# Half of the prompt rows' output projection moves into the attention of the sample rows, half between attention and merge

## The chip, the core and the metric

The kernel runs on one core of a Trainium2 chip. The metric is the device time of one execution in microseconds (us); before the change its median over three runs is 3195.66 us (3191.10 to 3197.16). The engines are called by their short names: PE multiplies matrices (PEld loads its stationary operand), DVE is the vector engine, ACT the scalar engine, POOL the general one, and SP issues all DMA transfers of this kernel, in the order in which they stand in its queue.

## The reference, cut to what matters

One layer of an encoder runs over two requests with the same weights, a prompt of 512 rows and a sample of 1024 rows. Each row goes through a mixer with two branches, and then through a feed-forward network:

```python
att = diff_attention(q, k, v, lam, rel_bias)          # softmax over all rows of the same request
att = rmsnorm(att, subln_w) * (1.0 - lam_init)         # per head
y_ssm = rmsnorm(y, ssm_norm_w)                         # the other branch
g = jax.nn.sigmoid(gates.reshape(b, S, 2, D_MODEL))
merged = g[:, :, 0] * (att @ w_proj_attn) + g[:, :, 1] * (y_ssm @ w_proj_ssm)
m = merged @ w_out                                     # the output projection
x = x + rmsnorm(m, norm_post_mix)
h = rmsnorm(x, norm_pre_ffn)                           # goes into the feed-forward network
```

All of it is in float32. D_MODEL is 1024; there are 8 heads of 2 x 64 columns. `x`, `w_out` and the other weights come from memory and the two outputs go back there.

## The kernel before, in words

The 1536 rows are three chunks of 512: chunk 0 is the prompt, chunks 1 and 2 the sample. Each float32 operand of a large product is split into a rounded part and the rest (`split`, line 133: ACT writes the first, DVE or POOL subtracts for the second), and `gemm` (line 164) issues three matmuls for each 128 rows of the contracted dimension, at lines 167, 168 and 169. A product of 1024 x 1024 weights comes in panels of 256 columns (`split_panel`, line 147), of which two fit (tags `whi`, `wlo`, two buffers each); their raw halves go through two buffers of tag `wraw`.

Engines take their instructions in order. That order is not the order of the text alone: the framework places the instructions by dependences, program order and its own estimate of times, and what it decided is seen in the built program.

Around the change there are these stages, by the code of the kernel before:

- **Attention of the sample** (lines 800 to 869). `heads` runs 8 heads; each has 8 blocks of 128 query rows. For a block PE makes the scores (tile `s`, lines 293 and 294), DVE adds the bias and finds the minimum (296), ACT takes the exponential (299), DVE combines the two maps (302 to 304), PE transposes (308, tile `t`), ACT and DVE split the transposed map (311, 312), and PE multiplies it with the values (tile `o`, 256 columns wide). After 4 blocks ACT copies `o` to `av` (319), SP stores it to `att_d` (320), and a mean square follows later (`mean_square`, tile `ms`, lines 323 to 327).
- **Side work** (`side_work`, line 837) is a generator, and `run` (line 210) takes one step of it for each two steps of the attention (`RATIO` 0.5). It has 32 steps: 8 for the gated projection of the prompt's attention and 24 for the gated projection of the other branch. They write `part_d`; their matmuls go to the tile `f`, one PSUM buffer.
- **Scaling** (`att_scale`, line 330). From the mean squares of all heads DVE works out one factor for each row and head, PE transposes them (tile `rt`, 341), DVE copies (343), SP stores them to `r_d` (344).
- **Output projection of the prompt** (`out_proj`, line 1040, for `m0`): 4 panels of `w_out` times 4 blocks of rows, each 24 matmuls of 256 columns. Its operand is `part_d` of chunk 0, loaded and split by `load_merged` (line 886). ACT copies each result and takes its square sum (1048, 1050).
- **Merge of chunk 1** (`merge`, line 895). `load_att` (346) loads for each of 8 heads the attention result and its factors from `r_d` (351, 349; three buffers `araw`), multiplies (352) and splits. Then 8 blocks of 24 matmuls of 512 columns, each gated and added to `part_d` (905 to 913).
- **Norms of chunk 0** (`norms`, line 1053): two normalizations of the projected prompt rows (1066, 1067, 1068, 1074), 32 transposes (1078), ACT evictions (1080) and stores to `h2_d`, beside the next output projection (`m1`). Merge and projection of chunk 2 and the feed-forward network follow.

Of the kernel before, what the change touches and what calls it, by code (L numbers as in the profile page):

```python
# [10 lines left out]
F32 = mybir.dt.float32  # L11
I32 = mybir.dt.int32
F32R = mybir.dt.float32r
AF = mybir.ActivationFunctionType
ALU = mybir.AluOpType
# [3 lines left out]
P = 128  # L19
D = 1024  # L20
KB = D // P
# [12 lines left out]
OT = ("gt", 2)  # L34
NG = 2
YE = ("act_pool",) * 4
RATIO = 0.5
QS = 0
IA = 1
AHEAD = (0,)  # L40
# [37 lines left out]
def hybrid_trunk_kernel(ctx: ExitStack, tc: tile.TileContext, a: dict, y_prompt, y_sample):  # L78
# [5 lines left out]
    def f(ap):  # L84
        return ap.bitcast(F32)
# [26 lines left out]
    r_d = [dram.tile([32 * n, P], F32, name=f"r_d{n}") for n in (1, 2)]  # L112
    m_d = dram.tile([D, 512], F32, name="m_d")
    part_d = dram.tile([D, T], F32, name="part_d")
    x2_d = dram.tile([T, D], F32, name="x2_d")
    h2_d = dram.tile([D, T], F32, name="h2_d")
    ff_d = [dram.tile([DFF, 768], F32, name=f"ff_d{g}") for g in range(2)]
# [29 lines left out]
    def split_panel(*srcs, eng="act_dve"):  # L147
        hi = wp.tile([P, KB, 256], F32R, tag="whi", name="whi")
        lo = wp.tile([P, KB, 256], F32R, tag="wlo", name="wlo")
        n = 256 // len(srcs)  # L150
        for s in (slice(0, 4), slice(4, 8)):
            raw = rp.tile([P, 4, 256], F32, tag="wraw", name="wraw")
            for i, src in enumerate(srcs):
                load(out=raw[:, :, i * n:(i + 1) * n], in_=src.rearrange("(a p) c -> p a c", p=P)[:, s])
            split(hi[:, s], lo[:, s], raw[:], eng)
        return hi, lo
# [173 lines left out]
    def att_scale(g, zq, msq, pool, psp, ptag):  # L330

        n = zq.shape[-1]
        r, t = [pool.tile([P, 8, n], F32, tag=t_, name=t_, bufs=1) for t_ in ("att_r", "att_t")]
        V.reciprocal(t, zq)
        V.tensor_mul(zq, msq, t)
        V.tensor_mul(zq, zq, t)
        V.tensor_scalar(zq, zq, 1.0, EPS, op0=ALU.mult, op1=ALU.add)
        rsqrt(r[:], zq[:], msq[:])
        V.tensor_mul(r, r, t)
        ps = psp.tile([P, 512], F32, tag=ptag, name="rt")  # L340
        TE.transpose(ps[0:8 * n, 0:P], r[:].rearrange("p h j -> p (h j)"), ident)
        rt = pool.tile([P, P], F32, tag="att_rt", name="rt", bufs=1)
        V.tensor_copy(rt[0:8 * n], ps[0:8 * n, 0:P])
        store(out=r_d[g][:], in_=rt[0:8 * n])
# [452 lines left out]

    ap = ctx.enter_context(tc.tile_pool(name="ap", bufs=1, reuse_waits="tile"))
    zq, msq = [ap.tile([P, 8, 8], F32, name=n) for n in ("zq", "msq")]
    with ExitStack() as ph2:  # L800
        qr = ph2.enter_context(tc.tile_pool(name="qr", bufs=2, reuse_waits="tile"))
        qk = ph2.enter_context(tc.tile_pool(name="qk", bufs=2, reuse_waits="tile"))
        pp = ph2.enter_context(tc.tile_pool(name="pp", bufs=2, reuse_waits="tile"))
        at = ph2.enter_context(tc.tile_pool(name="at", bufs=2, reuse_waits="tile"))
        yt = ph2.enter_context(tc.tile_pool(name="yt", bufs=2, reuse_waits="tile"))
        s_ps = ph2.enter_context(tc.tile_pool(name="s_ps", bufs=2, space=PSUM, reuse_waits="tile"))
        t_ps = ph2.enter_context(tc.tile_pool(name="t_ps", bufs=2, space=PSUM, reuse_waits="tile"))
        o_ps = ph2.enter_context(tc.tile_pool(name="o_ps", bufs=1, space=PSUM, reuse_waits="tile"))
        f_ps = ph2.enter_context(tc.tile_pool(name="f_ps", bufs=1, space=PSUM, reuse_waits="tile"))

        pend = []
        def panel(w_):
            w = wp.tile([P, 2, KB, P], F32R, tag="whi", name="whi")
            raw = rp.tile([P, KB, P], F32, tag="wraw", name="wraw")
            load(out=raw, in_=w_.rearrange("(a p) c -> p a c", p=P))
            split(w[:, 0], w[:, 1], raw[:], "act_dve")
            return w[:, 0], w[:, 1]

        def gated(r0, g0, cs, w, act):
            gt = yt.tile([P, 512], F32, tag="gt", name="gt")  # L820
            load(out=gt, in_=g_d[g0 + r0:g0 + r0 + P, cs])
            S.activation(out=gt, in_=gt, func=AF.Tanh, scale=0.5)
            ps = f_ps.tile([P, 512], F32, tag="f", name="f")
            gemm_fm(ps, w, slice(0, P), act)
            V.scalar_tensor_tensor(gt, gt, 1.0, ps, op0=ALU.add, op1=ALU.mult)
            return gt

        def y_rows(c):
            if c == NCH:
                return []  # L830
            v = yT_d[:, c * 512:(c + 1) * 512].rearrange("(a p) t -> p a t", p=P)
            raws = [wp.tile([P, 4, 512], F32, tag="wlo", name="yraw") for _ in range(2)]
            for raw, k in zip(raws, (0, 4)):
                load(out=raw, in_=v[:, k:k + 4])
            return raws

        def side_work():
            ahead = y_rows(0)
            aTt = yt.tile([P, 2, KB, 512], F32R, tag="yT", name="aTt", bufs=1)
            load_att(0, (aTt[:, 0], aTt[:, 1]), lambda: [t_[:, i] for t_ in [rp.tile([P, 2, 512], F32, tag="wraw", name="wraw")]  # L840
                                                 for i in range(2)])
            for r0 in range(0, D, P):
                gt = gated(r0, 0, slice(0, 512), panel(a["w_proj_attn"][0][:, r0:r0 + P]), (aTt[:, 0], aTt[:, 1]))
                store(out=m_d[r0:r0 + P, :], in_=gt)
                yield

            for c in range(NCH):
                cs = slice(c * 512, (c + 1) * 512)
                yTt = yt.tile([P, 2, KB, 512], F32R, tag="yT", name="yTt", bufs=1)
                for i_, raw in enumerate(ahead):  # L850
                    for j in (0, 2):
                        k = i_ * 4 + j
                        split(yTt[:, 0, k:k + 2], yTt[:, 1, k:k + 2], raw[:, j:j + 2], YE[k // 2])
                ahead = y_rows(c + 1)
                for r0 in range(0, D, P):
                    gt = gated(r0, D, cs, panel(a["w_proj_ssm"][0][:, r0:r0 + P]), (yTt[:, 0], yTt[:, 1]))
                    if c == 0:
                        mt = rp.tile([P, 512], F32, tag="wraw", name="mt")
                        load(out=mt, in_=m_d[r0:r0 + P, :])
                        G.tensor_add(gt, gt, mt)  # L860
                    store(out=part_d[r0:r0 + P, cs], in_=gt)
                    yield

        side = side_work()
        run(heads(512, 1024, range(8), pend, zq, msq, qk, pp, at, qr, s_ps, t_ps, o_ps),
            side, RATIO)
        for _ in side:
            pass
        pend.pop()()


    with ExitStack() as ph3:
# [9 lines left out]

        def big_pair():
            return [big.tile([P, KB, 512], F32R, tag="big", name="big") for _ in range(2)]

        def load_merged(c):
            hi, lo = big_pair()
            for k in range(0, KB, 2):
                both = mp.tile([P, 2, 512], F32, tag="mt", name="both", bufs=4)
                load(out=both, in_=part_d[k * P:(k + 2) * P, c * 512:(c + 1) * 512].rearrange("(a p) t -> p a t", p=P))  # L890
                S.activation(out=hi[:, k:k + 2], in_=both, func=AF.Copy, scale=0.5)
                V.scalar_tensor_tensor(lo[:, k:k + 2], both, 0.5, f(hi[:, k:k + 2]), op0=ALU.mult, op1=ALU.subtract)
            return hi, lo

        def merge(c, aTt):
            cs = slice(c * 512, (c + 1) * 512)
# [138 lines left out]
        with ExitStack() as ph3a:  # L1035
# [4 lines left out]
            def out_proj(mT):  # L1040
                tiles = [mp.tile([P, D], F32, tag="mt", name="mt", bufs=4) for _ in range(4)]
                sums = wk.tile([P, 4, 4], F32, tag="ms4", name="ms4")
                for p0 in range(0, D, 256):
                    w = split_panel(a["w_out"][0][:, p0:p0 + 256])
                    for j in range(4):
                        ps = mm_tile(256)
                        gemm_tm(ps, w, mT, slice(j * P, (j + 1) * P))
                        S.copy(tiles[j][:, p0:p0 + 256], ps)
                        sq = wk.tile([P, 256], F32, tag="gt", name="msq")
                        S.activation(out=sq, in_=ps, func=AF.Square, accum_out=sums[:, j, p0 // 256:p0 // 256 + 1])  # L1050
                return tiles, sums
# [32 lines left out]
                return load_att(c, big_pair(), lambda: [  # L1084
                    wk.tile([P, 512], F32, tag="araw", name="araw", bufs=3) for _ in range(2)])

            m0 = load_merged(0)
            att_scale(1, zq, msq, ap, tr_ps, "tr")
            aT1 = att(1)
            t0 = out_proj(m0)  # L1090
            m1 = merge(1, aT1)
            norms(0, t0)
            aT2 = att(2)
# [118 lines left out]
```

## Time and profile before

| | us |
|---|---|
| median of 3 runs | 3195.66 |
| profiled execution | 3197.76 |
| its span, first to last instruction | 3196.0 |
| PE busy in the span | 3044.8 (95%) |
| DVE busy | 1837.5 (57%) |
| ACT busy | 1256.7 (39%) |

The share of PE is that of the whole program; the stages around the change differ from it, and so the rows below take them one by one. A PE row's duration holds the pipeline's depth, so matmuls overlap: what a matmul costs in a stream is the distance from one start to the next. The granted clock of PE is given as a share of 2.4 GHz.

### The profile page before, as it was taken

How to read it: one execution, taken by the hardware profiler on the slowest of the kernel's cores; microseconds unless marked ns; L12 is line 12 of the kernel's file. 1: busy time of each engine (PE TensorE's matmuls, PEld its weight loads, DVE VectorE, ACT ScalarE, POOL GpSimd, SP SyncE). 2: the span in 40 equal slices, each digit the busy share in tenths (PEclk: the TensorE clock that was granted, in tenths of full speed). 3: DMA queues.
4: the chain of work that ended last, by engine and by line, in shares of the span. 5: the costliest groups of instructions: out<-in, count | busy, mean ns of one | idle time of the engine just before them, and what ended most of it. 6: DMA issues, size and time to landing. Idle time of an engine off the chain costs nothing. (4 is left out here: it accounts for less than half of the span.)

```text
span 3196.0 us, 44151 instructions
## 1 busy us (share of the span) xinstructions
PE 3044.8 (95%) x16667; PEld 2677.0 (84%) x16667; DVE 1837.5 (57%) x2953; ACT 1256.7 (39%) x2301; POOL 681.7 (21%) x520
## 2 busy tenths in 40 slices
PE   8999999999999999899999898978999899989998
PEld 7988887888887777788888787878999899978787
DVE  5214444455327996387878955686667765632444
ACT  4103333333303333366666645543333333332343
POOL 0001111000133442243332100023333433210100
PEclk9999999999999999999999999989999999999999
DMA  4633333123554444755546047644333333363454
GB/s 149 195 99 113 112 104 106 57 79 106 152 170 136 147 143 149 212 173 167 165 137 186 27 139 239 218 141 136 103 98 105 97 103 91 114 203 97 124 163 132
DMA packets 443165, 430.35 MB, mean 135 GB/s; under 512 B 25232, under 2 KB 360305, under 8 KB 441841
## 3 DMA queue, kind: packets, MB, share of 16 engines
q1 hardware_dynamic: 442953, 427.55, 43.3%
q8 instruction: 131, 2.15, 0.3%
q14 instruction: 81, 0.66, 0.1%
HBM read 315.40 MB, written 120.44 MB: 136 GB/s over the span
## 5 line engine op out<-in xcount | busy, mean ns | idle before, releaser
L167 PE MATMUL acc<-hT,whi 128*128 128x512 f32 x1056 | 421.4, 399 | 4.0 <-ACT st L453 4.0
L168 PE MATMUL acc<-hT,whi 128*128 128x512 f32 x1056 | 416.7, 395 | 0.0
L169 PE MATMUL acc<-hT,wlo 128*128 128x512 f32 x672 | 262.2, 390 | 0.0
L167 PEld LDWEIGHTS acc<-hT,whi 128*128 128x128 f32 x1056 | 199.0, 188 | 50.2 <-issue 5.8
L299 ACT ACTIVATE pt<-pt,nm 128x1024 f32<-128x1024 f32 (+1 forms) x192 | 193.1, 1006 | 109.9 <-DVE nm L296 106.6
L168 PEld LDWEIGHTS acc<-hT,whi 128*128 128x128 f32 x1056 | 199.1, 189 | 42.7 <-issue 3.6
L296 DVE CUSTOM_DVE_ANT_0 pt<-s,tb 128x1024 f32<-128x1024 f32 (+1 forms) x192 | 197.5, 1041 | 52.4 <-PE s L294 40.4
L167 PE MATMUL acc<-whi,hT 128*128 128x256 f32 x768 | 225.2, 293 | 1.2 <-DVE st L374 0.6
L169 PE MATMUL acc<-whi,hT 128*128 128x256 f32 x768 | 225.6, 294 | 0.5 <-DVE hT L207 0.3
L168 PE MATMUL acc<-wlo,hT 128*128 128x256 f32 x768 | 224.2, 292 | 0.0
L169 PE MATMUL d<-dhi,fl 128*128 128x512 f32 x528 | 207.8, 393 | 8.9 <-DVE fl L136 8.9
L167 PE MATMUL d<-dhi,fh 128*128 128x512 f32 x528 | 207.7, 393 | 6.8 <-ACT fh L135 6.8
L168 PE MATMUL d<-dlo,fh 128*128 128x512 f32 x528 | 207.1, 392 | 0.0
L135 ACT CAST whi<-wraw 128x1024 fp32r<-128x1024 f32 (+1 forms) x115 | 115.9, 1036 | 213.8 <-PE acc L169 83.1
L136 DVE TENSOR_TENSOR fl<-raw,fh 128x896 fp32r<-128x896 f32 (+1 forms) x72 | 86.0, 1195 | 198.1 <-ACT fh L135 190.2
L234 POOL TENSOR_TENSOR ql<-raw,qh 128x512 fp32r<-128x512 f32 x48 | 65.3, 1373 | 577.3 <-ACT qh L231 567.9
L167 PE MATMUL mm<-op,wy 128*128 128x384 f32 x528 | 178.8, 339 | 9.5 <-ACT op L135 7.3
L169 PE MATMUL mm<-op,wy 128*128 128x384 f32 x528 | 178.6, 338 | 0.0
L168 PE MATMUL mm<-op,wy 128*128 128x384 f32 x528 | 178.3, 338 | 0.0
L136 DVE TENSOR_TENSOR wlo<-wraw,whi 128x1024 fp32r<-128x1024 f32 x80 | 97.1, 1243 | 114.9 <-ACT whi L135 105.6
L135 ACT CAST fh<-raw 128x896 fp32r<-128x896 f32 (+1 forms) x72 | 70.8, 983 | 225.8 <-PE d L168 189.9
L167 PEld LDWEIGHTS acc<-whi,hT 128*128 128x128 f32 x768 | 148.3, 193 | 12.1 <-issue 10.0
(358 smaller groups left out, 8325.0 us busy)
## 6 DMA issues: line engine op xcount, KB each, us to landing
wraw<-in_w_in_dram SPq DMA_DIRECT2D x60, 512.0 KB
wraw<-in_w_gate_up_dram SPq DMA_DIRECT2D x92, 256.0 KB
raw<-ff_d SPq DMA_DIRECT2D x48, 448.0 KB
wr<-in_w_gate_up_dram SPq DMA_DIRECT2D x80, 256.0 KB
ff_d<-c SPq DMA_DIRECT2D x88, 192.0 KB
g_d<-st SPq DMA_DIRECT2D x48, 256.0 KB
xg<-xs_d SPq DMA_DIRECT2D x48, 256.0 KB
gt<-g_d SPq DMA_DIRECT2D x48, 256.0 KB
```

The costliest lines, as they stand in the source:

```text
L135: S.copy(hi, raw)
L136: V.tensor_sub(lo, raw, f(hi))
L167: TE.matmul(ps, ah, bh, start=(i == 0), stop=False)
L168: TE.matmul(ps, ah, bl, start=False, stop=False)
L169: TE.matmul(ps, al, bh, start=False, stop=(i == n - 1))
L234: G.tensor_sub(q_l[:, s_], q_r[:, s_], f(q_h[:, s_]))
L296: V.tensor_tensor_reduce(out=pt[:], in0=sps[:], in1=tb[:, off:off + SL], scale=-1.0, scalar=3.0e38, op0=ALU.add, op1=ALU.min, accum_out=nm ...
L299: S.activation(out=pt, in_=pt, func=AF.Exp, bias=nm[:, m:m + 1], scale=-1.0, accum_out=(z0, zs[:, 0:1])[m])
```

## The change

Eight of the sixteen row-and-panel blocks of the prompt's output projection become side steps that write to the PSUM tile `f`, eight more (`LATE`) write to buffers of the scores' tile `s` under the name `late`. The attention takes 0.625 side steps for each of its own. The result goes to a new tensor `mo_d` in memory, and is loaded from there when its norms are due; `out_proj` is no longer called for chunk 0. The mean square of the last head and the scaling of the attention stand in the text ahead of the rest of the side work. `load_merged` is gone; its loads and splits stand in `side_work`.

```diff
-RATIO = 0.5
+RATIO = 0.625
+LATE = 8
+    mo_d = dram.tile([512, D], F32, name="mo_d")
+    sums0 = ap.tile([P, 4, 4], F32, name="sums0")
...
+            m0 = yt.tile([P, 2, KB, 512], F32R, tag="yT", name="m0", bufs=1)
+            for k in range(0, KB, 2):
+                both = rp.tile([P, 2, 512], F32, tag="wraw", name="both")
+                load(out=both, in_=part_d[k * P:(k + 2) * P, 0:512].rearrange("(a p) t -> p a t", p=P))
+                S.activation(out=m0[:, 0, k:k + 2], in_=both, func=AF.Copy, scale=0.5)
+                V.scalar_tensor_tensor(m0[:, 1, k:k + 2], both, 0.5, f(m0[:, 0, k:k + 2]), op0=ALU.mult, op1=ALU.subtract)
+            for i in range(16):
+                p0, j = i // 4 * 256, i % 4
+                if j == 0:
+                    w = split_panel(a["w_out"][0][:, p0:p0 + 256])
+                if i < 16 - LATE:
+                    ps = f_ps.tile([P, 512], F32, tag="f", name="f")[:, 0:256]
+                else:
+                    ps = s_ps.tile([P, 1024], F32, tag="s", name="late")[:, 0:256]
+                gemm_tm(ps, w, (m0[:, 0], m0[:, 1]), slice(j * P, (j + 1) * P))
+                mo = yt.tile([P, 512], F32, tag="gt", name="mo")
+                S.copy(mo[:, 0:256], ps)
+                S.activation(out=mo[:, 256:512], in_=ps, func=AF.Square, accum_out=sums0[:, j, i // 4:i // 4 + 1])
+                store(out=mo_d[j * P:(j + 1) * P, p0:p0 + 256], in_=mo[:, 0:256])
+                yield
...
+        pend.pop()()
+        att_scale(1, zq, msq, ap, t_ps, "t")
         for _ in side:
             pass
-        pend.pop()()
...
-            m0 = load_merged(0)
-            att_scale(1, zq, msq, ap, tr_ps, "tr")
             aT1 = att(1)
-            t0 = out_proj(m0)
+            t0 = [mp.tile([P, D], F32, tag="mt", name="mt", bufs=4) for _ in range(4)], sums0
+            for j, mt in enumerate(t0[0]):
+                load(out=mt, in_=mo_d[j * P:(j + 1) * P, :])
```

In the built program PE's order is the same up to the last gated side step. The eight `f` blocks of the projection stand behind it among the last two and a half heads, the first of them behind 24 more score matmuls. Six of the `late` blocks stand behind the last scores, among the last transposes and value products. Lines of the changed kernel are two higher up to line 860, and more behind.

PE at the end of the attention, before: the last value product, the last mean square, the first matmuls of the output projection (`mm<-whi,big`).

```order
L167 MATMUL o<-aT,vh 128x256
L168 MATMUL o<-aT,vh 128x256
L169 MATMUL o<-aT,vl 128x256
L326 MATMUL ms<-onec,av 128x1 x4
L167 MATMUL mm<-whi,big 128x256
L168 MATMUL mm<-wlo,big 128x256
```

PE at the same place now: the end of the last `late` block (the last 47 `late` matmuls stand behind the last value product), the mean square, the transposed factors, the merge (`mm<-big,whi`).

```order
L169 MATMUL late<-whi,m_15511 128x256
L170 MATMUL late<-wlo,m_15511 128x256
L171 MATMUL late<-whi,m_15511 128x256
L328 MATMUL ms<-onec,av 128x1 x4
L343 MATMUL rt<-ident,att_r 64x128
L169 MATMUL mm<-big,whi 128x512 x4
L170 MATMUL mm<-big,whi 128x512
L171 MATMUL mm<-big,wlo 128x512
```

What stood between the mean square and the merge was the whole projection, 384 matmuls with `rt` among them; now only `rt` stands there. The merge goes through four blocks at once, head by head (12 matmuls for each head), where before it went block by block.

SP from the last stores of the attention's result to the first loads of the factors, before (`pt` and `gt` belong to the merge):

```order
L320 DMA att_d<-av 128x512 x3
L349 DMA araw<-att_d 128x512
L907 DMA pt<-part_d 128x512
L320 DMA att_d<-av 128x512
L344 DMA r_d_82<-rt 64x128
L351 DMA araw<-r_d_82 128x512
L349 DMA araw<-att_d 128x512
```

SP now, from the last store of the attention's result (`xr` are input rows, `pmw` a norm's weights, `mt` the projected prompt rows):

```order
L322 DMA att_d<-av 128x512
L924 DMA pt<-part_d 128x512
L922 DMA gt<-g_d 128x512
L886 DMA mo_d<-mo 128x256 x2
L1055 DMA pmw<-in_norm_post_mix_dram 128x1024
L1107 DMA mt<-mo_d 128x1024 x4
L156 DMA wraw<-in_w_proj_attn_dram 128x4x256 x2
L1082 DMA xr<-in_x_prompt_dram 128x512 x2
L346 DMA r_d_82<-rt 64x128
L353 DMA araw<-r_d_82 128x512
```

The store of the factors stood right behind the last store of the attention's result; now two small stores and nine loads stand between the two.

DVE around the copy of the factors to `rt`, before:

```order
L186 SCALAR_TENSOR_TENSOR att_r<-msq,att_r 128x64
L339 TENSOR_TENSOR att_r<-att_r,att_t 128x64
L343 COPY rt<-rt 64x128
L352 SCALAR_TENSOR_TENSOR araw<-araw,cols 128x512
L136 TENSOR_TENSOR big<-araw,big 128x512
```

DVE at the same place now:

```order
L1083 SCALAR_TENSOR_TENSOR mt<-mt,mr,pmw 128x512 x2
L188 SCALAR_TENSOR_TENSOR att_r<-msq,att_r 128x64
L1083 SCALAR_TENSOR_TENSOR mt<-mt,mr,pmw 128x512 x2
L341 TENSOR_TENSOR att_r<-att_r,att_t 128x64
L1083 SCALAR_TENSOR_TENSOR mt<-mt,mr,pmw 128x512 x2
L345 COPY rt<-rt 64x128
L1083 SCALAR_TENSOR_TENSOR mt<-mt,mr,pmw 128x512 x2
L1084 TENSOR_TENSOR mt<-mt,xr 128x512 x2
L354 SCALAR_TENSOR_TENSOR araw<-araw,cols 128x512
```

The first six products of the prompt's norms, which read three of the four loaded `mt`, moved ahead of the copy of the factors; before they stood behind the merge's first panels.

## Rows read from the trace of the kernel before

**Rows 1.** Stretches: busy us by engine, (x) instructions, granted clock, DMA share, GB/s.

```profile
1414.00:1600.00 186.00, 181.30 (x1005) 153.14 (x1004) 149.03 (x237) 118.70 (x190) 70.97 (x44) 0.99 0.58 173
1730.00:1842.00 112.00, 98.40 (x619) 85.02 (x617) 100.38 (x178) 75.85 (x130) 18.56 (x12) 0.95 0.26 80
1842.00:1848.00 6.00, 1.78 (x10) 1.57 (x9) 0.00 (x0) 2.82 (x4) 0.00 (x0) 0.71 0.40 126
...
1945.00:2004.00 59.00, 51.43 (x397) 49.80 (x396) 23.86 (x41) 29.31 (x69) 0.00 (x0) 0.94 0.58 185
```

**Rows 2.** Groups on PE, 1730 to 1842 us: busy us, mean ns, idle before.

```profile
L293 PE MATMUL s<-km,qh 128*128 128x512 f32 x69 | 29.6, 430 | 4.2 <-DVE nm L296 3.8
...
L167 PE MATMUL o<-aT,vh 128*128 128x256 f32 x88 | 27.7, 315 | 6.4 <-ACT aT L311 5.7 <-DVE zs L302 0.7
...
L308 PE MATMUL t<-ident,pt 128*128 128x128 f32 x168 | 25.4, 280 | 1.9 <-DVE aT L312 1.4 <-DVE msq L327 0.5
```

**Rows 3.** A group on PE, 1414 to 1600 us: gated side work.

```profile
L167 PE MATMUL f<-yTt,whi 128*128 128x512 f32 x113 | 45.7, 404 | 0.1
```

**Rows 4.** Timeline of PE: start us, duration us; a stream of each width.

```profile
1562.51 0.39 PE L169 MATMUL f<-yTt,whi 128*128 128x512 f32 x1
1562.74 0.39 PE L167 MATMUL f<-yTt,whi 128*128 128x512 f32 x1
...
1568.34 1.04 PE L308 MATMUL t<-ident,pt 128*128 128x128 f32 x8
...
1890.18 0.28 PE L168 MATMUL mm<-wlo,big 128*128 128x256 f32 x1
1890.30 0.28 PE L169 MATMUL mm<-whi,big 128*128 128x256 f32 x1
```

**Rows 5.** Timeline of DVE: two splits of a weight panel in a row.

```profile
1867.86 2.35 DVE L136 TENSOR_TENSOR wlo<-wraw,whi 128x1024 fp32r<-128x1024 f32 x2
```

**Rows 6.** Timeline of PE, then SP: the end of the attention, the factors.

```profile
1841.95 0.28 PE L169 MATMUL o<-aT,vl 128*128 128x256 f32 x1
1846.45 1.87 PE L326 MATMUL ms<-onec,av 128*128 128x1 f32 x8 [4.22 <-ACT av L323]
...
1857.33 0.47 SPq L344 DMA_DIRECT2D r_d<-rt  x1
1859.95 0.32 SPq L351 DMA_DIRECT2D araw<-r_d  x1
```

**Rows 7.** Timeline of DVE: factors copied; heads 1, 3, 4 and 8 scaled.

```profile
1857.02 0.28 DVE L343 COPY rt<-rt 64x128 f32<-64x128 f32 x1 [0.66 <-PE rt L341]
1863.21 0.75 DVE L352 SCALAR_TENSOR_TENSOR araw<-araw,cols 128x512 f32<-128x512 f32 x1 [5.91 <-DMA araw<-r_d]
...
1871.38 0.75 DVE L352 SCALAR_TENSOR_TENSOR araw<-araw,cols 128x512 f32<-128x512 f32 x1 [0.56 <-DMA araw<-r_d]
...
1877.46 0.75 DVE L352 SCALAR_TENSOR_TENSOR araw<-araw,cols 128x512 f32<-128x512 f32 x1 [3.95 <-DMA araw<-r_d]
...
1895.38 0.75 DVE L352 SCALAR_TENSOR_TENSOR araw<-araw,cols 128x512 f32<-128x512 f32 x1 [1.81 <-DMA araw<-r_d]
```

**Rows 8.** Timeline of PE: first matmul behind merge 1, behind projection 1.

```profile
1944.84 0.28 PE L167 MATMUL mm<-whi,big 128*128 128x256 f32 x1
...
2006.46 0.40 PE L167 MATMUL mm<-big,whi 128*128 128x512 f32 x1
```

**Rows 9.** Waits on PE, 1729.8 to 2004 us: total us, times, longest.

```profile
PE mm L167 <- ACT msq L1050: 3.7, 1, 3.7
```

**Rows 10.** Stretches with much DMA traffic, and the clock after a pause.

```profile
1330.00:1360.00 30.00, 25.29 (x100) 19.49 (x100) 12.63 (x18) 12.76 (x16) 15.07 (x11) 0.94 0.93 254
...
1972.00:1974.00 2.00, 0.00 (x0) 0.00 (x0) 0.00 (x0) 1.55 (x5) 0.00 (x0) 1.00 0.99 350
...
1976.00:1978.00 2.00, 2.00 (x11) 2.00 (x10) 0.00 (x0) 1.27 (x6) 0.00 (x0) 0.50 0.83 318
```

**Rows 11.** DMA transfers: destination and source, count, KB each.

```profile
pmw<-in_norm_post_mix_dram SPq DMA_DIRECT2D x1, 512.0 KB
```

More of the change, by code (lines that the diff above doesn't have):

```diff
@@ L884, in big_pair @@
             return [big.tile([P, KB, 512], F32R, tag="big", name="big") for _ in range(2)]
[L886 to L893, printed above, removed]
         def merge(c, aTt):
```

## The prediction

> **What bounds the kernel now.** I read the busy time by stretches first, since the share of PE over the whole span says nothing of the stages the change touches. While gated side work lies beside the attention, PE is busy 181.3 of 186 us; from the last side step to the end of the attention it is busy 98.4 of 112 us, while DVE is busy 100.4 [rows 1]. So the attention is bound by PE early and by DVE late. Busy time flatters PE, as matmuls overlap. The timeline gives what one costs in a stream: 0.23 us for 512 columns, 0.12 us for 256 columns, and 0.11 us for a transpose ((1.04 - 0.28) / 7) [rows 4]. With these, PE's need from 1730 to 1842 us is 139 score matmuls (69 in the row shown, 70 in its twin) x 0.23 + 264 value matmuls (three groups of 88) x 0.12 + 168 transposes x 0.11 + the other 48 of the 619 records, mean squares, x 0.12 = 32.0 + 31.7 + 18.5 + 5.8 = 88 us [rows 1, 2, 4]. So 24 of the 112 us are room. That room is what half of the projection is to fill.
>
> Then the timelines across the seam. The last value product starts at 1841.95; PE waits 4.2 us for the mean square's input; the factors are copied to `rt` at 1857.0, stored at 1857.3, and the first load of them starts 2.6 us later, when the store has landed [rows 6, 7]. Head 1 is scaled at 1863.2, which is 21.3 us behind the last value product, and head 8 at 1895.4: 32.2 us for seven heads, 4.6 us each, as each waits for a load [rows 7]. PE feels none of this, because the prompt's projection, 384 x 0.12 = 46 us, stands in between. The merge ends at 1944.8, that is 102.9 us behind the last value product, and the next projection ends at 2006.5, 61.6 us later, though its 384 matmuls and 32 transposes need only 46.1 + 3.5 = 49.6 us [rows 4, 8]. The waits name the longest loss there: 3.7 us for a free PSUM buffer, whose eviction on ACT stood behind those of the norms' transposes [rows 9]; part of the rest is a slower clock, 0.94 on average there [rows 1].
>
> **The change part by part.** PE has the same matmuls as before. What can change is waiting, so I count three stretches against those times.
>
> *The attention's tail.* All 16 blocks less the last 47 matmuls stand ahead of the last value product: 337 x 0.12 = 40.4 us more for PE. If the whole room of 24 us is filled, the tail grows by 40.4 - 24 = 16.4 us; if none is, by 40.4. Neither end is likely. In the built order 24 of the 139 score matmuls stand ahead of the first new block, so roughly 24/139 of the 112 us, 19 us, has nothing to fill it. Behind that I take the rate PE reached when side work was always at hand: in 1414 to 1600 us the 1005 records are 337 side matmuls and 180 of scores (0.23 us each), 264 of values and 48 of mean squares (0.12) and 176 transposes (0.11), 176 us of need in 186, or 94% [rows 1, 3, 4], where one of the three side groups is shown. The tail's need of 88 + 40.4 = 128.4, less some 16 in the first 19 us, is 112.4, which at 94% takes 119.6; with the first 19 us, 138.6 instead of 112, or **27 us more**. DVE is not the limit: it gains 10 weight halves and 4 operand pieces ahead of the end, 14 x 1.18 = 16.5 us [rows 5], which with its 100.4 makes 117. The ACT work added (two evictions for each block) lies beside that too. If that cover went, the upper end holds it.
>
> *From the last value product to the end of the merge.* PE now has the 47 `late` matmuls, 5.6 us, and then waits for head 1. Two orders decide when that comes. On DVE six products of the prompt's norms stand ahead of the copy of the factors, and they need three of the four `mt` loads. On SP the store of the factors stands behind `pmw`, four `mt`, two weight halves (512 KB each) and two `xr` (256 KB each): 4 MB (the size of one [rows 11], the others by their shapes). These loads can begin when the last `late` block is out and stored, about 6.5 us behind the last value product. At 254 GB/s, the rate of a stretch with 0.93 of the DMA engines' time taken, 4 MB needs 16.5 us; at the 350 GB/s of two full microseconds elsewhere 12 us [rows 10]. Then 2.6 us for the store to land and 3.3 for the load of head 1 [rows 6, 7]: head 1 is scaled at 24.4 to 28.9 us, where it was 21.3. I take 27. The seven further heads keep their 4.6 us (weight loads stood among them before, input rows and stores of `x2_d` do now): head 8 at 59.2. Its scaling and split take about 1.4 us more, its 12 matmuls 12 x 0.23 = 2.8. Until then four of the eight blocks of the merge are done, as they advance head by head; the other four need a new weight panel split (1.2 us, the first half of it) and 96 x 0.23 = 22.1 us. Sum: 59.2 + 1.4 + 2.8 + 1.2 + 22.1 = 86.7 against 102.9: **16 us less**. The low end lets nothing stand in front (head 1 at 21.3) and heads come every 4.0 us (4.1 is the distance over the first three): 21.3 + 28 + 27.5 = 76.8, 26 us less. The high end has head 1 at 29 and all heads at the 6.1 us of the pair that had 1 MB of weights between them [rows 7]: 29 + 42.7 + 27.5 = 99.2, 4 us less.
>
> In this stretch the granted clock matters too. In the trace a stretch of 2 us without a matmul is followed by one at 0.50, the level of 1.2 GHz, with 11 matmuls of 256 columns in 2 us [rows 10]; yet the tail, with its many short waits, has 0.95 [rows 1]. Between two heads PE would idle 4.6 - 2.8 = 1.8 us. The Trainium skill (TensorE: Matmul & The Clock Gate, section HAM oscillation — how this bites in real kernels) says that a loop whose compute for one slice is shorter than the wait for the next drops the clock at every slice. By that rule each head's matmuls would run at the low level, and the stretch would be that of the second rival; by the tail's row they would not, and the sum above holds. I keep the row.
>
> *The next projection.* Its norms no longer wait for their DVE work beside the merge's evictions, and 12 of the 32 transposes moved into the merge, where PE waits anyway. Of the 12 us lost there (61.6 - 49.6) between nothing and all can return. 20 transposes with their evictions and stores are still between its matmuls, so I take **8 us less**.
>
> Sum: +27 - 16 - 8 = +3 us, with ends of 16.4 - 26 - 12 = -22 and 40.4 - 4 - 0 = +36. The profiled execution took 3197.8, 2.1 above the median of the runs; so the profile would read about 3201 and the median 3195.7 + 3 = 3199. What can be told from no change for this kernel is about 0.2%, 6.4 us. My forecast is no measurable change: PE's wait moves from the tail to the gap ahead of the merge.
>
> **The rivals.**
> 1. *The tail is filled better than the early attention.* If PE finds work at 98% there, the tail grows by 112.4 / 0.98 + 19 - 112 = 22 us; with loads at the fast rate the merge's end moves up by 20 (head 1 at 24.4, heads every 4.3), and the projection gives 10: 22 - 20 - 10 = -8, 3188. For it: the new blocks lie where DVE, not PE, sets the pace, and the loads of `mt` are long rows. Against it: the order of DVE, and a single PSUM buffer `f` for eight of the blocks.
> 2. *The clock falls between the heads.* Then 12 matmuls take twice 2.8, 5.6 us, more than the 4.6 of a head; eight heads from 27 + 1.4 end at 73.2 instead of 63.4, 10 us later: 3199 + 10 = 3209. It decides from the point where most heads find PE at the low level.
> 3. *The tail's room stays room.* Blocks of the projection have to wait for weight halves behind two `wraw` buffers in SP's queue, and DVE's splits of them hold up the attention behind them: with half of the room left unused the tail grows by 40.4 - 12 = 28 beside the 5 us that its first part cannot use, 33 in all, and if head 1 comes at 29 the merge gives 14 and the projection 7: +12, 3208. For it: DVE runs in order and is busy 90% there. Against: beside the early attention, with a weight split for every side step, PE reached 94%.
>
> That the change would not do what it says can be left out: in the built order the eight blocks stand inside the attention.
>
> **How the numbers follow.** No measurable change (3199, within 6.4 us of 3196) 0.41; rival 1 0.27; rival 2 0.11; rival 3 0.21. Faster by over 0.2% is rival 1, slower is rivals 2 and 3. The predicted time is 3199. The forecast's own range is 3190 to 3202; the range that leaves out a tenth on either side reaches past rival 1 towards the low end, 3183, and past rivals 2 and 3, 3215, within the bounds of the three terms (3174 to 3232).
>
> **What would show it.** The last value product at 1858 to 1882 us instead of 1842; an idle gap of PE of about 20 us between the last `late` matmul and the first of the merge; head 1 some 27 us behind the last value product; `r_d` stored behind `mt`; four blocks of the merge in steps of about 4.6 us; the next projection in 50 to 57 us. I am wrong if the tail hardly grows (then faster), if the granted clock between heads is near 0.5, or if the gap ahead of the merge is under 12 or above 30 us.

## The result and the profile after

The changed kernel takes 3215.93 us (median of 4 runs, 3212.82 to 3218.66), the kernel before on the same chip 3194.05 us: ratio 1.0064, 95% interval [1.0049, 1.0079]. It is slower, by some 20 us; the forecast was no measurable change, and the median lies 0.9 us above the upper end of the range. The profiled execution has a span of 3211.0 us, 15.0 more than before.

Four stretches hold all of it: the tail (last gated side matmul to last value product), the gap (to the first matmul of merge 1), the merge, the next projection. Their rows, of the kernel before, then of the changed one (columns as in [rows 1]):

```profile
1729.20:1842.00 112.80, 99.20 (x622) 85.69 (x620) 100.75 (x178) 76.22 (x130) 18.56 (x12) 0.95 0.25 80
1842.00:1895.80 53.80, 49.58 (x395) 49.37 (x395) 22.81 (x40) 23.08 (x55) 0.00 (x0) 0.94 0.42 133
1895.80:1944.80 49.00, 45.77 (x194) 37.05 (x193) 39.74 (x65) 25.27 (x51) 0.00 (x0) 0.97 0.79 269
1944.80:2006.50 61.70, 54.13 (x418) 52.47 (x418) 23.99 (x41) 30.04 (x72) 0.00 (x0) 0.94 0.57 182
```

```profile
1725.30:1866.30 141.00, 131.46 (x943) 120.02 (x942) 114.89 (x189) 96.43 (x184) 18.37 (x12) 0.99 0.31 98
1866.30:1895.30 29.00, 7.21 (x58) 6.66 (x57) 13.57 (x43) 7.71 (x17) 0.00 (x0) 0.67 0.75 251
1895.30:1957.30 62.00, 52.63 (x204) 41.01 (x205) 39.48 (x65) 21.72 (x37) 0.00 (x0) 0.90 0.70 220
1957.30:2021.20 63.90, 52.86 (x406) 51.40 (x405) 21.97 (x27) 29.96 (x71) 0.00 (x0) 0.92 0.53 172
```

The tail is 28.2 us longer, the gap 24.8 shorter, the merge 13.0 longer, the projection 2.2 longer: 18.6 in all. The tail also began 3.9 us earlier; what follows the projection takes 1189.8 us against 1189.5. 18.6 - 3.9 + 0.3 = 15.0, the difference of the spans.

The timeline across the seam answers to [rows 6 and 7]. First PE, then SP, then DVE:

```profile
1866.25 0.28 PE L171 MATMUL o<-aT,vl 128*128 128x256 f32 x1
...
1871.79 0.28 PE L171 MATMUL late<-whi,m 128*128 128x256 f32 x1
1872.64 1.05 PE L328 MATMUL ms<-onec,av 128*128 128x1 f32 x8 [0.57 <-ACT av L325]
1884.78 0.39 PE L343 MATMUL rt<-ident,att_r 128*64 128x128 f32 x1 [11.09 <-DVE att_r L341]
1895.32 1.22 PE L169 MATMUL mm<-big,whi 128*128 128x512 f32 x2 [10.15 <-ACT big L137]
```

```profile
1875.69 2.02 SPq L1107 DMA_DIRECT2D mt<-mo_d  x4
1877.81 1.30 SPq L156 DMA_DIRECT2D wraw<-in_w_proj_attn_dram  x2
1879.16 3.19 SPq L1082 DMA_DIRECT2D xr<-in_x_prompt_dram  x2
1886.17 0.47 SPq L346 DMA_DIRECT2D r_d<-rt  x1
1889.91 0.33 SPq L353 DMA_DIRECT2D araw<-r_d  x1
```

```profile
1881.62 1.41 DVE L1083 SCALAR_TENSOR_TENSOR mt<-mt,mr,pmw 128x512 f32<-128x512 f32 x2 [0.90 <-DMA mt<-mo_d]
...
1885.88 0.27 DVE L345 COPY rt<-rt 64x128 f32<-64x128 f32 x1
...
1893.81 0.75 DVE L354 SCALAR_TENSOR_TENSOR araw<-araw,cols 128x512 f32<-128x512 f32 x1 [3.44 <-DMA araw<-r_d]
...
1898.72 0.75 DVE L354 SCALAR_TENSOR_TENSOR araw<-araw,cols 128x512 f32<-128x512 f32 x1 [1.10 <-DMA araw<-r_d]
...
1905.18 0.75 DVE L354 SCALAR_TENSOR_TENSOR araw<-araw,cols 128x512 f32<-128x512 f32 x1 [3.30 <-DMA araw<-r_d]
```

DVE's products of the norms (L1083) stand around the chain of the factors; the store of `r_d` on SP stands behind `mt`, the weight halves and `xr`; head 1 is scaled 27.6 us behind the last value product (21.3 before). Heads 1, 2 and 3 are shown; head 8 is scaled at 1928.28, 34.5 us behind head 1, 4.9 us a head. Merge and projection end at 1957.31 and 2021.19 (before [rows 8]). PE's largest waits from 1725 to 2030 us, the last of which answers to [rows 9]:

```profile
PE mm L169 <- ACT big L137: 16.5, 4, 10.1
PE rt L343 <- DVE att_r L341: 11.1, 1, 11.1
PE s L295 <- DVE nm L298: 4.9, 6, 1.5
PE mm L169 <- ACT big L929: 3.9, 2, 2.3
PE mm L169 <- ACT msq L1067: 3.7, 1, 3.7
```

Two are new: PE waits for the heads' operands (`big`, L137) and for the factors (`att_r`).

### The profile page after: what moved, and what is told of

Its sections match the earlier page's. It is cut to its first block, busy times and chain, and to the rows that moved or that the text cites. A ratio compares the mean times of both kernels' runs of the same rounds, so it can differ in the third digit from the quotient of the medians.

```text
span 3211.0 us, 44186 instructions
## 1 busy us (share of the span) xinstructions
PE 3033.6 (94%) x16667; PEld 2663.5 (83%) x16667; DVE 1837.7 (57%) x2953; ACT 1256.7 (39%) x2301; POOL 681.5 (21%) x520
## 5 line engine op out<-in xcount | busy, mean ns | idle before, releaser
L298 DVE CUSTOM_DVE_ANT_0 pt<-s,tb 128x1024 f32<-128x1024 f32 (+1 forms) x192 | 197.3, 1041 | 55.2 <-PE s L296 40.8
L171 PE MATMUL d<-dhi,fl 128*128 128x512 f32 x528 | 207.7, 393 | 10.8 <-DVE fl L138 10.8
L137 ACT CAST whi<-wraw 128x1024 fp32r<-128x1024 f32 (+1 forms) x115 | 115.8, 1036 | 211.3 <-PE acc L170 83.3
L137 ACT CAST fh<-raw 128x896 fp32r<-128x896 f32 (+1 forms) x72 | 70.7, 983 | 224.5 <-PE d L170 203.7
```

The source lines that it names most:

```text
L137: S.copy(hi, raw)
L171: TE.matmul(ps, al, bh, start=False, stop=(i == n - 1))
L298: V.tensor_tensor_reduce(out=pt[:], in0=sps[:], in1=tb[:, off:off + SL], scale=-1.0, scalar=3.0e38, op0=ALU.add, op1=ALU.min, accum_out=nm ...
```

## The experiments

Theory: the tail has room for a part of the new work only; what is taken out behind it comes back incompletely, as three waits that 46 us of projection used to cover now show: the factors, the heads one by one, the merge's evictions. Rivals: the clock between the heads; DVE and late weight halves in the tail; the norms' new place.

All runs in one table. Stretches are from one profile each, by the same four points; us and ratio are medians against the kernel before on the same chip.

| kernel | tail | gap | merge | projection | sum | us | ratio [95%] |
|---|---|---|---|---|---|---|---|
| before | 112.8 | 53.9 | 49.0 | 61.6 | 277.3 | | |
| changed | 141.0 | 29.1 | 62.0 | 63.9 | 295.9 | 3215.9 | 1.0064 [1.0049, 1.0079] |
| all behind | 114.2 | 53.8 | 46.9 | 62.5 | 277.4 | 3195.7 | 1.0013 [1.0000, 1.0025] |
| late behind | 129.8 | 28.5 | 68.9 | 59.8 | 287.0 | 3203.5 | 1.0031 [1.0019, 1.0043] |
| one panel | 137.3 | 29.5 | 63.3 | 60.0 | 290.1 | 3210.1 | 1.0040 [1.0027, 1.0053] |
| factors first | 139.4 | 22.8 | 68.5 | 60.1 | 290.8 | 3209.2 | 1.0048 [1.0033, 1.0064] |
| raw heads | 140.4 | 31.8 | 48.5 | 57.4 | 278.1 | 3197.2 | 1.0003 [0.9990, 1.0015] |
| partial sums | 139.9 | 27.5 | 67.5 | 54.1 | 289.0 | 3207.3 | 1.0038 [1.0024, 1.0052] |
| both buffers | 139.7 | 30.9 | 48.0 | 52.3 | 270.8 | 3194.3 | 1.0002 [0.9988, 1.0016] |
| both, factors first | 140.1 | 24.5 | 48.3 | 58.7 | 271.5 | 3192.4 | 0.9998 [0.9985, 1.0011] |
| both, late behind | 127.5 | 28.8 | 47.2 | 64.2 | 267.7 | 3179.1 | 0.9955 [0.9940, 0.9971] |
| the same, DVE evicts | 129.9 | 28.2 | 47.0 | 61.7 | 266.8 | 3187.8 | 0.9971 [0.9958, 0.9984] |
| before, both buffers | 113.2 | 53.9 | 43.6 | 55.2 | 265.9 | 3181.6 | 0.9966 [0.9952, 0.9980] |

Where each stretch goes is read from its row; what an edit is worth, from the ratio, since what follows the projection takes 1187.3 to 1197.6 us in these profiles. A stretch has its own spread: kernels that have the same matmuls in the tail differ there by 1.6 us (139.4 to 141.0, six kernels) and 2.4 us (127.5 to 129.9, three).

### How many blocks the tail takes

All behind: all sixteen blocks are issued behind the last value product (`issue_after` puts what it encloses behind that instruction).

```diff
-RATIO = 0.625
-LATE = 8
+RATIO = 0.5
+LATE = 16
...
-        for _ in side:
-            pass
+        with tc.issue_after(last_o[-1].ins):
+            for _ in side:
+                pass
```

> The changed kernel with all sixteen blocks behind the last value product and the side work's share of PE back at the value of before: the code of the change stays, only its filling of the attention's tail is undone. Theory (the tail is where the time is lost: blocks put there take nearly as long as they save behind it): the tail about 112 us as in the kernel before, the merge's end about 103 us behind the last value product, with 46 us of blocks in the gap, time 3193 to 3201. Rival (the loss lies in the new place of the norms' loads and products, which this kernel keeps): 3206 or above. Rival (half of the blocks in the tail do bring something): this kernel is slower than the changed one.

The theory held: tail 114.2, merge's end 100.7 us behind the last value product, 1.0013. The loss comes with the blocks that left the gap for the tail. The new place of the norms, which this kernel keeps, costs at most 0.25% (the interval is 1.0000 to 1.0025) as long as 46 us of blocks lie over it.

Late behind: the same without the first four changed lines: eight blocks in the tail, eight behind.

> The eight blocks of the second half now stand on PE behind the last value product instead of in the attention's last blocks; all else as in the changed kernel. Theory (the loss is half-blocks pushed into a tail that has no room for them, while PE idles behind it): the last value product at about 1845 to 1852 us instead of 1866, so a tail of 120 to 127 us instead of 141; behind it 192 matmuls of 0.12 us, 23 us, which fill the gap of 24 us up to head 1; head 1 some 21 to 28 us behind the last value product, as now; the merge's end 10 to 20 us earlier than in the changed kernel; time 3196 to 3206. Rival (the tail grows because DVE and the late weight halves hold the attention, not PE): the tail stays at 135 us or more, and the time is 3216 or above, as the late work then comes on top. Rival (a slower clock between the heads makes the loss): the merge is as long as now counted from its first matmul and the time falls by under 4 us.

The time is as the theory had it, the tail 3 us above its range; 0.33% faster than the changed kernel. The 23 us of blocks fill the gap but for its end: PE is busy 23.9 of its 28.5 us and then waits 4.6 us, by the profile for ACT's eviction of a block. But the merge's end, counted from the tail's start, came only 5 us earlier, not 10 to 20: the heads were scaled 6.0 us apart instead of 4.9, and the merge took 68.9 us. The three kernels with 0, 192 and 337 side matmuls ahead of the last value product have tails of 114.2, 129.8 and 141.0 us: the first 192 (23.0 us of PE at 0.12) cost 15.6 us, the next 145 (17.4 us) 11.2. A microsecond put there costs 0.64 to 0.68 us from the first block on; the last blocks are no worse than the first.

One panel: is it PE or the weights?

```diff
-                if j == 0:
+                if i == 0:
                     w = split_panel(a["w_out"][0][:, p0:p0 + 256])
```

> The changed kernel, but all sixteen side blocks use the first panel of weights: the loads, casts and splits of the other three panels are left out (six halves of 512 KB, six of the DVE splits), and so is what they would have computed. All matmuls stay. Theory (the tail grows because PE's matmuls fill it: 40 us of new work into 24 us of room): the tail keeps 137 to 141 us, time 3211 to 3217. Rival (late weight halves and DVE's splits hold up the tail): the tail falls by 5 us or more, to 136 or less, time 3210 or less.

The tail, 137.3 us, is at the lower edge of the theory's; the time is at the rival's bound, its interval overlapping that of the changed kernel. With 8.6 us less of DVE work the tail is 3.7 us shorter. It also has 13 `late` matmuls less, 1.6 us of PE's work: 60 of them stand behind the last value product here, 47 in the changed kernel.

```profile
1729.40:1866.70 137.30, 129.48 (x930) 119.14 (x929) 106.25 (x183) 89.77 (x175) 19.27 (x12) 0.98 0.25 80
```

So late halves and splits are at most 2 to 4 of the 28 us. PE is busy 129.5 of 137.3 us: it is PE's own queue that is full.

### What holds the merge

Factors first: the loads of the norms are issued behind the first load of the factors.

```diff
-            load(out=pmw, in_=a["norm_post_mix"].broadcast_to([P, D]))
...
-            for j, mt in enumerate(t0[0]):
-                load(out=mt, in_=mo_d[j * P:(j + 1) * P, :])
+            with tc.issue_after(first_rb[1, 0].ins):
+                load(out=pmw, in_=a["norm_post_mix"].broadcast_to([P, D]))
+                for j, mt in enumerate(t0[0]):
+                    load(out=mt, in_=mo_d[j * P:(j + 1) * P, :])
```

> The loads of the prompt's norms (the weight row and the four rows of outputs) are issued only behind the first load of the factors; all else as in the changed kernel. Theory (head 1 is late because the norms' loads on SP and their products on DVE stand ahead of the factors): the copy of the factors on DVE right behind its transpose, head 1 some 20 to 23 us behind the last value product instead of 27.5, the merge's end 5 us earlier, time about 3211, if the next projection does not give it back by the norms' own lateness; 3214 to 3217 if it does. Rival (head 1 waits for the DMA of the factors themselves, whatever stands ahead): head 1 stays at 26 us or more, no change.

Head 1 comes at 21.3 us as expected, and the merge ends at 91.2, where it was: the second half of the theory fell. DVE's rows show why: head 2 comes 9.1 us behind head 1, with eight operations of the norms between (the last three are shown):

```profile
1885.53 0.75 DVE L356 SCALAR_TENSOR_TENSOR araw<-araw,cols 128x512 f32<-128x512 f32 x1 [6.04 <-DMA araw<-r_d]
...
1892.67 2.07 DVE L1084 SCALAR_TENSOR_TENSOR mt<-mt,mr,pmw 128x512 f32<-128x512 f32 x3
1894.66 0.74 DVE L356 SCALAR_TENSOR_TENSOR araw<-araw,cols 128x512 f32<-128x512 f32 x1
...
1899.32 0.75 DVE L356 SCALAR_TENSOR_TENSOR araw<-araw,cols 128x512 f32<-128x512 f32 x1 [0.78 <-DMA araw<-r_d]
```

A head needs two of three `araw` buffers, one for the raw head and one for its factors, so each waits for the one before, as the next run shows. The last head decides, not the first.

Raw heads: the eight raw heads get the one `big` buffer that is free there.

```diff
-                return load_att(c, big_pair(), lambda: [
-                    wk.tile([P, 512], F32, tag="araw", name="araw", bufs=3) for _ in range(2)])
+                araw = lambda: wk.tile([P, 512], F32, tag="araw", name="araw", bufs=3)
+                if c > 1:
+                    return load_att(c, big_pair(), lambda: [araw(), araw()])
+                raws = big.tile([P, KB, 512], F32R, tag="big", name="raws")
+                each = iter(range(KB))
+                return load_att(c, big_pair(), lambda: [f(raws[:, next(each), :]), araw()])
```

> The eight raw heads that the merge scales first have a buffer of their own, loaded early; the three load buffers then hold only the factors. All else as in the changed kernel. Theory (the heads come 4.9 us apart because each waits for a load into one of three buffers): the heads scaled 1.5 to 3 us apart, the merge then goes at PE's own pace, 192 matmuls of 0.23 us, and ends 60 to 70 us behind its first operand instead of 63.5 to 62 only if the second panel is late; the end of the merge 8 to 16 us earlier, time 3200 to 3208. Rival (the clock between the heads sets the merge): no wait for heads is left, the clock is 1.0 there too, and the gain is as large; told apart by the gap: if the heads come fast and the merge's matmuls still take over 0.3 us each, it is the clock. Rival (the three DMA queues' time, not the buffers): the heads stay 4 us or more apart and the time does not change.

Heads 1, 2, 3, then 4 to 6 in one row, and the eighth:

```profile
1893.55 0.75 DVE L354 SCALAR_TENSOR_TENSOR raws<-raws,cols,araw 128x512 f32<-128x512 f32 x1 [2.10 <-DMA araw<-r_d]
1894.66 0.75 DVE L354 SCALAR_TENSOR_TENSOR raws<-raws,cols,araw 128x512 f32<-128x512 f32 x1 [0.36 <-DMA araw<-r_d]
1896.64 0.75 DVE L354 SCALAR_TENSOR_TENSOR raws<-raws,cols,araw 128x512 f32<-128x512 f32 x1 [1.22 <-DMA araw<-r_d]
1900.32 2.08 DVE L354 SCALAR_TENSOR_TENSOR raws<-raws,cols,araw 128x512 f32<-128x512 f32 x3
...
1908.26 0.75 DVE L354 SCALAR_TENSOR_TENSOR raws<-raws,cols,araw 128x512 f32<-128x512 f32 x1
```

The eighth comes 14.7 us behind the first, so 2.1 us a head, less than the 2.8 that PE needs for one, and the merge takes 48.5 us instead of 62.0, though head 1 is 2.7 us later than in the changed kernel; its end comes 80.3 us behind the last value product instead of 91.1. This one edit gives back all that the change lost, 1.0003. The clock rival falls as a cause of its own: the granted clock in the gap is the same 0.67, and the merge's matmuls take 48.5 / 192 = 0.25 us each, where the rival asked for over 0.3.

### What holds the projection

Partial sums: the free `big` buffer holds the partial sums instead.

```diff
+            pts = big.tile([P, KB, 512], F32R, tag="big", name="pts") if c == 1 else None
...
-                    pt = wk.tile([P, 512], F32, tag="pt", name="pt", bufs=1)
+                    pt = f(pts[:, kb, :]) if c == 1 else wk.tile([P, 512], F32, tag="pt", name="pt", bufs=1)
```

> The prompt's partial sums, which the merge's evictions add, have eight slots instead of one; all else as in the changed kernel. Theory (the next projection did not gain because the evictions of the merge come one by one, 7 us apart, each behind a load into the single slot, and end 21 us behind the merge): the evictions end within 8 us of the merge's end, PE waits less for free banks in the projection, which takes 54 to 60 us instead of 63.9; time 3208 to 3212. Rival (the projection is held by the transposes of the normed rows and their evictions on ACT, behind which its own evictions stand): the merge's evictions end earlier and the projection still takes 62 us or more; time 3214 to 3217.

The projection takes 54.1 us, 9.8 less, and PE's waits in it fall from 11.1 to 5.3 us. But the merge is 5.5 us longer, and the evictions still end 18.6 us behind it (21.5 in the changed kernel, 19.8 before), not within 8. Counted from the last value product they end no earlier than in the changed kernel: at 113.6 us, against 112.6. So the single slot costs PE some waits, but it is not what makes the evictions late. Of the 9.8 us, 5.8 are left at the projection's end, counted the same way; by the ratio the gain is not certain, as the intervals overlap a little (1.0038 and 1.0064).

### Together

Both buffers: one buffer, first for the raw heads and then, block by block, for the partial sums (`pt = f(raws[:, kb, :])`).

> The changed kernel with the spare buffer used twice: for the eight raw heads, and, when these are scaled, for the prompt's partial sums that the merge's evictions add. Theory (heads one by one cost 11 us of the merge, the single slot of the partial sums 10 us of the projection, and the two add up): the merge's end 80 us behind the last value product, the projection in 54 us, time 3193 to 3197. Rival (one wait takes the other's place, as the next late thing is the transposes' evictions either way): the projection 57 us or more as with the heads' buffer alone, time 3197 to 3200.

The stretches are as the theory said (78.9 and 52.3 us), and 7.3 us shorter in sum than with the raw heads alone; the ratio, 1.0002, does not show that gain. Half of it goes behind the projection, in 1194.1 us against 1190.2; why, these runs don't tell.

Both, factors first:

> The changed kernel with the spare buffer used twice, and with the norms' loads behind the first load of the factors. With the factors first alone head 1 came 6 us earlier and the merge's end did not. Theory (that gain was taken by the heads' own pace behind it, so with the raw heads loaded early it shows): head 1 at 20 to 24 us behind the last value product instead of 29.4, the merge's end at 70 to 74 us instead of 78.8, the projection 52 to 58 us, time 3186 to 3192, against 3194 with the buffer alone. Rival (what the norms lose by their late loads is as much): the merge's end as theory says, but the projection 59 us or more, 3193 to 3198.

Now head 1's gain reaches the merge's end (72.8 us, 6.1 earlier), and the projection takes 6.4 us longer, between theory and rival: a wait that changed places, no gain.

Both, late behind:

> As the kernel with the spare buffer used twice, and the eight late blocks behind the last value product. Theory (the three losses are independent): tail 130 us, the merge's end 78 to 84 us, the projection 54 us, 13 us less in all than the kernel before: 3181 to 3188. Rival (behind the last value product a chain of loads sets the merge's end, not PE's work: then the late blocks, put there, only move it back): the merge's end 90 us or more and 3190 to 3196.

The lowest ratio, 0.9955, ahead of the two kernels above; the intervals of the two below overlap with its own. Tail and merge as the theory had them or better; the projection missed, at 64.2 us. The last two stretches:

```profile
1875.10:1922.30 47.20, 46.27 (x192) 37.52 (x193) 40.01 (x68) 21.76 (x37) 0.00 (x0) 0.96 0.97 335
1922.30:1986.50 64.20, 53.70 (x417) 51.86 (x416) 28.33 (x49) 32.38 (x78) 0.00 (x0) 0.89 0.56 183
```

PE is busy through the whole merge, and the DMA engines are at 0.97 of their time, 335 GB/s.

The same, DVE evicts: every second eviction of the normed rows on DVE.

```diff
+                    if c == 0 and k % 2:
+                        V.tensor_scalar(hr, ps, cols[:, C_FFN + k:C_FFN + k + 1], 0.0, op0=ALU.mult, op1=ALU.add)
```

> The kernel with late blocks and the spare buffer used twice, with every second eviction of the prompt's normed rows on DVE instead of ACT. Theory (in that kernel the next projection takes 64 us, as eight of these evictions on ACT stand ahead of its own, and PE waits 4.3 us for a free bank there): the projection 57 to 61 us, time 3173 to 3178. Rival (it waits for the merge's last evictions and for the stores that free the evicted rows' buffers): still 62 us or more, no change from 3179, or more, where DVE holds the merge's evictions behind them.

The theory missed: 61.7 us and no gain in time. PE's longest wait there, for an eviction of the projection on ACT, fell from 4.3 to 2.0 us, and the projection by 2.5, so ACT's evictions hold it by that and not more. That its loads and stores are late behind the full DMA of the merge is what the row above suggests; it was not tried by itself.

Before, both buffers: the same buffers without the change.

> The kernel before, with the spare buffer used twice in the same way: shows what the buffers are worth without the change. Theory (in the kernel before, the 46 us of the projection cover the heads, so only the evictions can gain): the merge's end 99 to 103 us behind the last value product, the projection 54 to 57 us instead of 61.6, time 3187 to 3192. Then the change, with its waits taken away, is worth the distance to the run with late blocks and buffers: 3 to 8 us. Rival (the projection is held by the norms' transposes there): no gain, 3194 to 3198.

0.9966: the gain is larger than expected, and lies in the merge (43.6 us) as well as in the projection (55.2). Against the kernel with late blocks behind (0.9955), the intervals overlap: with the waits gone, the change is worth nothing that these runs can tell. By stretches it costs 14.3 us in the tail, brings 21.5 up to the merge's end, and costs 9.0 in the projection.

## Why the forecast failed, point by point

**The tail, +27.** Measured +28.2, or 30 if one counts that the last gated side step now stands some 2 us of scores and transposes later in the attention. The mechanism was the one given, PE: in the changed kernel it is busy 131.5 of 141.0 us, and the work worked out for it was 128.4; before, 99.2 of 112.8 for 88. The growth is 40 us of work less 10 to 12 of the 24 us of room. DVE grew to 114.9 us, as counted (117); 8.6 us less of it (one panel) shortened the tail by 4 us at most.

**Last value product to the merge's end, -16.** Measured -11.8, the right mechanism mis-sized by 4.2. Head 1 at 27.6 us (27); seven heads in 34.5 us (32.2); from head 8 to the end 29.0 (27.5). The prediction had the pace in its sum, 4.6 us a head [rows 7] where PE needs 2.8. What it did not draw from it is that the pace, more than head 1, is the price: it was in the trace of before, costing nothing, as the projection lay over it.

**The next projection, -8.** Measured +2.3: this is the step that failed, and 10.3 of the 15.7 us by which the sum missed. It rested on the norms' DVE work leaving the merge's evictions. That work left, but there was little of it, and another wait came in its place. From the merge's end to the last eviction DVE's busy time fell from 16.9 to 14.9 us, yet the stretch grew from 19.9 to 21.6. Between these evictions DVE also scales the heads of chunk 2, the next one to be merged, which come through the same three `araw` buffers. DVE's waits in that stretch, 1957.3 to 1978.9 us, in the changed kernel:

```profile
DVE araw L354 <- DMA araw<-r_d: 4.9, 3, 2.1
DVE gt L928 <- DMA pt<-part_d: 1.5, 2, 0.8
DVE big L930 <- ACT big L929: 1.4, 2, 0.7
```

Before, the heads cost DVE 0.4 us in that stretch and the partial sums 1.2. PE's waits in the projection went from 7.5 to 11.1 us; the one that the prediction had named, for `msq`, has the same 3.7 [rows 9]. That the partial sums' single slot made the evictions late, as the run with eight slots supposed, did not come out. That the heads of chunk 2 do is read from these waits; no run changed them alone, so their share in the 10.3 us stays open.

**The rivals.** Rivals 2 and 3 foretold a slower kernel (3209 and 3208), each by a cause that is not the one found. Rival 3 named DVE and late weights in the tail: these are 4 us at most. Rival 2 needed most heads at the low level. The clock did fall beside the waits for the heads, but not for most of them. The granted clock of PE from the gap to head 8 (1928):

```profile
1890.00:1894.00 4.00, 0.00 (x0) 0.50 0.60 203
1894.00:1900.00 6.00, 4.68 (x11) 0.50 0.80 265
1900.00:1906.00 6.00, 3.40 (x14) 0.97 0.76 248
1906.00:1912.00 6.00, 5.37 (x16) 0.72 0.78 240
1912.00:1918.00 6.00, 3.21 (x13) 0.95 0.55 189
1918.00:1924.00 6.00, 6.00 (x22) 0.77 0.53 149
1924.00:1930.00 6.00, 4.85 (x26) 1.00 0.49 134
```

Head 1's matmuls run at 0.50, the level of 1.2 GHz; later stretches lie between 0.72 and 1.00. From head 8 to the end there are 1.5 us more than worked out, which suggests that slower matmuls had mostly been made up before the last head came. The Trainium skill (TensorE: Matmul & The Clock Gate, HAM oscillation — how this bites in real kernels) says that the clock drops at every slice of a loop whose compute for one slice is shorter than the wait for the next. By the prediction's own figures a head is not such a slice, with 2.8 us of matmuls against a wait of 1.8 (2.1 as measured, 4.9 - 2.8), so its step from there to a drop at every head was a misreading. The trace agrees with the section for head 1, whose matmuls follow a wait of 10 us; what happened at the later heads, drops in part, it does not cover.

**What would show it.** The last value product (1866), head 1 at 27, `r_d` behind `mt` and heads in steps of 4.9 us came as listed; PE's gap of 23 us between the last `late` matmul and the merge as well (20 foretold). The projection in 50 to 57 us did not.

## What to carry to other kernels

Before work is taken out from between two stages, list every wait it covers, with its pace and not only its first item, and count as gain only what is left when each is on the path: here a load chain of 4.9 us a head held the merge's end back by 10.8 us, and the same chain of the next chunk stood among the evictions. Filler behind a stage pays while the next operands are on their way: 23 us of it left PE a wait of 4.6 us in a gap of 28.5. These runs do not show that more is too much: 46 us there was no worse than 23, neither while the heads came slowly (1.0013 and 1.0031) nor with the buffers (0.9966 and 0.9955). Each microsecond of filler in the tail cost 0.64 to 0.68. And try the freed buffer alone first: it was worth 0.34% without the change.

## What was not expected of the hardware

The DMA traffic in the merge of the kernel with both buffers and late blocks behind reached 335 GB/s at 0.97 of the DMA engines' time over 47 us, near the 350 of two microseconds in [rows 10]; there a shorter merge was followed by a longer projection. And the tail begins between 1718.8 and 1729.9 us in the eleven profiles of the changed kernel and its variants, whose instructions stand in the same order up to there: 11 us of spread, more than most of the edits are worth, so that stretches, not absolute times, had to be compared.
